# The first four feed-forward units: each second product in a PSUM bank of its own, and weight tiles ordered behind the norm of the second token half

## The chip, the core and the metric

One core of one Trainium2 chip runs the whole program in one launch. The metric is device microseconds for one execution. The profile is one execution taken by the hardware profiler; its times count from the first instruction.

## What is computed

One residual block of a streaming encoder over 512 tokens of width 1024, in float32:

```python
xn = rmsnorm(h, norm_mix_g)
u  = xn @ w_in                                  # q, k, v, rnn_x, rnn_gate, gate_a, gate_b
ya = chunked_band_attention(q, k, v, rel_table) @ w_attn_out
yb = (rg_lru(conv(xr)) * gelu(gr)) @ w_rnn_out
h  = h + (g_a * ya + g_b * yb) @ w_o
hn = rmsnorm(h, norm_ffn_g)
g, up = split(hn @ w_ffn_in)                    # 1024 -> 2 x 2816
h  = h + (silu(g) * up) @ w_ffn_out
out = rmsnorm(h, final_norm_g)
```

## The kernel before

Every matrix product is done on values split into a high part (rounded to the matmul's type, by a ScalarE copy) and a low part (the rest, by a VectorE subtraction): `mm3` issues three matmuls, high by high, high by low, low by high (lines 76, 77, 78).

The products with `w_ffn_in` are cut further, in the manner of Strassen and Winograd. A *unit* is 256 columns of the output (named fg0, fu0, fg2, fu2, fg4, ...; g is the gate half, u the other). Its weight block gives four quarter blocks and four sums of them (a11, a12, a22, s1 to s4 are the seven used); the normed activations give quarter blocks b11, b21, b22 and four sums t1 to t4. A unit is then seven *products* of 512 by 128 by 256, each twelve matmuls of 128 x 128 x 256, in place of eight.

Units from fg4 on go one after the other through `block_product`. The first four (fg0, fu0, fg2, fu2; `ahead_names`) go side by side: first a11 b11 and a12 b21 for each of the four, then s4 b22 for the four, then s1 t1, s2 t2, s3 t3, a22 t4, four products each time. This lets TensorE begin on b11 and b21, which need the first half of the tokens alone, while the second half is still being normed. I write s4(2) for the product s4 b22 of the third of these units, counted from 0. For each of the four units `firsts` holds a PSUM tile p, in which a11, s2, s3 and a22 accumulate, and an SBUF tile c of the four quarters of its output. The products a12, s4 and s1 go to another PSUM tile q and are taken from there into c.

*PSUM.* There are eight banks; the pools give four to the tag `mm` (the p tiles), two to the tag `t` and two to the tag `s`. `of_pair` gives one q tile of `s`, one bank, to two units: the first unit writes the left half of that bank and the second the right half. A write to a bank waits until the reads of that bank which come before it in the program are over. The tag `t` serves the transposes of `turned`.

*Weight tiles.* The sums s1 to s4 of the first four units were written to HBM earlier. `first_tile` loads the parts of two units (a *pair*, 0 or 1) into one of three `raw` buffers by two DMAs on SyncE's queue (line 1068), copies the high part on ScalarE (L1070) and makes the low part on VectorE (L1071). The high and low parts lie in a `whl` buffer; four of these are in the pool `wp`, and the a11 and a12 blocks of the four units (one buffer a unit) hold all four until their products are done. `first_pair("s4", 0, ...)` and `first_pair("s4", 1, ...)` have places of their own (`sums_room`, `x32p`). I write s1/0 for the tile of s1 of pair 0.

*The norm and the turn.* `square_h`, `summed_h` and `scaled_h` make the normed rows xs of a token tile (sum of squares, square root on ScalarE at L1048, reciprocal and scaling on VectorE at L1053 and L1055); tiles 0 and 1 are the first token half, 2 and 3 the second. `turned(xs, jp, ...)` transposes two feature tiles of two token tiles into one bank of tag `t` (PE, L324) and reads them out: high part on ScalarE (L329), low part on VectorE (L330), and the plain values x32, half on each (L332, L334). For the second half, jp 0 and 2 give x32 alone, and jp 4 and 6 give b22 and x32. `right_sum` splits a sum t1 to t4 into its parts `bt` (L82, L83).

*Order.* In this part TensorE's instructions are issued in the order of the program text (`manual_schedule`). The other engines' queues are ordered by a planner that walks the program with its own model of times and takes, of what it thinks ready, the earliest in the text. `tc.issue_after(ins)` puts the instructions traced inside it, those on the engine of `ins`, behind `ins` in that engine's queue; it sets an order there and no wait on another engine.

Of the kernel before, what the change touches and what calls it, by code (L numbers as in the profile page):

```python
# [8 lines left out]
F32 = mybir.dt.float32  # L9
F32R = mybir.dt.float32r  # L10
AF = mybir.ActivationFunctionType
ALU = mybir.AluOpType
PSUM = bass.MemoryType.PSUM

P = 128
D = 1024
# [20 lines left out]
def block_kernel(ctx: ExitStack, tc: tile.TileContext, x, norm_mix_g, w_in, b_merge, rel_table,  # L37
# [3 lines left out]
    pe, dve, act, pool, sp = nc.tensor, nc.vector, nc.scalar, nc.gpsimd, nc.sync  # L41
# [4 lines left out]
    def opened(name, bufs=1, side="left"):  # L46
        st = ExitStack()
        return st, st.enter_context(pool_of(name, bufs, side))
# [14 lines left out]
    ps = ctx.enter_context(tc.tile_pool(name="ps", bufs=2, space=PSUM, reuse_waits="tile"))  # L63
# [4 lines left out]
    def f(ap):  # L68
        return ap.bitcast(F32)

    def mm_tile(name, tag="mm"):
        return ps.tile([P, S], F32, tag=tag, bufs=4 if tag == "mm" else 2, name=name)
# [22 lines left out]
    ahead_names = strassen[:4]  # L95
# [187 lines left out]
    eps_t = cp.tile([P, 1], F32, name="eps_t")  # L283
    dve.memset(eps_t[:], EPS)
    warm = cp.tile([P, 1], F32, name="warm")
# [7 lines left out]
    for n, w in enumerate((w_rg_r, w_rg_i)):  # L293
        pairs = w.rearrange("(t two) d e -> two d t e", two=2)
        for e in range(2):
            at = slice(HD * (n ^ e), HD * (n ^ e) + HD)
# [23 lines left out]
    def turned(xs, jp, g, dst, half, name, whole_of=None):  # L320
        pt = ps.tile([P, 2, 256], F32, tag="t", bufs=2, name=f"pt_{name}{half}_{jp}")
        for i in range(2):
            for j in range(2):
                pe.transpose(pt[:, j, i * P:(i + 1) * P], xs[i][:, (jp + j) * P:(jp + j + 1) * P], ident[:])  # L324
        for j in range(2):
            jj = jp + j
            hi, lo = dst(jj, 0, half), dst(jj, 1, half)
            if hi is not None:
                act.activation(hi, pt[:, j], AF.Identity, scale=g[:, jj:jj + 1])  # L329
                dve.scalar_tensor_tensor(lo, pt[:, j], g[:, jj:jj + 1], f(hi), ALU.mult, ALU.subtract)  # L330
            if whole_of and j == 0:
                act.activation(whole_of(jj, half), pt[:, j], AF.Identity, scale=g[:, jj:jj + 1])  # L332
            elif whole_of:
                dve.tensor_scalar(whole_of(jj, half), pt[:, j], g[:, jj:jj + 1], None, ALU.mult)  # L334

    def norm_half(pl, src, ssq, g, dst, half, name):
        xs = [scaled(pl, src, ssq, name, 2 * half + i)[0] for i in range(2)]
        for jp in range(0, KT, 2):
            turned(xs, jp, g, dst, half, name)
# [52 lines left out]
    gf = vc[:, V_GF:V_GF + 8]  # L392
# [244 lines left out]
    ss = ctx.enter_context(tc.tile_pool(name="ss", bufs=2, space=PSUM, reuse_waits="tile"))  # L637
# [244 lines left out]
    with tc.manual_schedule(engines={mybir.EngineType.PE}):  # L882
        chain, second = ([mm_tile(f"pv_{tag}{i}", tag) for i in range(2)] for tag in ("mm", "t"))
# [107 lines left out]
    for j in range(KT):  # L991
# [6 lines left out]
        at = lo_half if j % 4 < 2 else slice(0, S)  # L998
# [9 lines left out]
    ht = [zp.tile([P, D], F32, tag="z", name=f"h{t}") for t in range(NT)]  # L1008
# [25 lines left out]
            dve.scalar_tensor_tensor(hs, bank_of(2 * half + i, cc)[:], 0.5, hs, ALU.mult, ALU.add)  # L1034

    hsq, q2s = [], {}

    def square_h(t, cc):
        if t not in q2s:
            q2s[t] = cp.tile([P, 2], F32, tag="hsq2", bufs=2, name=f"hsq2_{t}")  # L1040
        junk = tg_.tile([P, S], F32, tag="tg", name=f"hj{t}_{cc}")
        act.activation(junk[:], ht[t][:, cc * S:(cc + 1) * S], AF.Square, accum_out=q2s[t][:, cc:cc + 1])

    def summed_h(t):
        q = cp.tile([P, 1], F32, tag="ssq", bufs=4, name=f"hsq{t}")
        dve.tensor_reduce(q[:], q2s[t][:], mybir.AxisListType.X, ALU.add)
        sd = cp.tile([P, 1], F32, tag="sd", bufs=4, name=f"sd_ffn{t}")
        act.activation(sd[:], q[:], AF.Sqrt, bias=eps_t[:], scale=1.0 / D)  # L1048
        return sd

    def scaled_h(t, sd):
        rs = cp.tile([P, 1], F32, tag="rs", bufs=4, name=f"rs_ffn{t}")
        dve.reciprocal(rs[:], sd[:])  # L1053
        o = x32p.tile([P, D], F32, tag="xs", bufs=2, name=f"xs_ffn{t}")
        dve.tensor_scalar(o[:], ht[t][:], rs[:, 0:1], None, ALU.mult)  # L1055
        return o

    def finish_h(t, cc):
# [5 lines left out]
    def first_tile(pl, tag, bufs, low, keys, srcs):  # L1064
        name = "_".join(keys[0])
        raw = wp.tile([P, 2, 4, P], F32, tag="raw", bufs=3, name=f"raw_{name}")
        for i, src in enumerate(srcs):
            sp.dma_start(out=raw[:, i], in_=src)
        o = pl.tile([P, 2, 2, 4, P], F32R, tag=tag, bufs=bufs, name=f"whl_{name}")
        act.activation(o[:, :, 0], raw[:], AF.Copy)  # L1070
        low.tensor_sub(o[:, :, 1], raw[:], f(o[:, :, 0]))  # L1071
        for i, key in enumerate(keys):
            first_w[key] = o[:, i]

    def first_block(name, half, kh):
        col = chunks[index[name]][1][0][1] + half * P
        return w_ffn_in[kh * S:(kh + 1) * S, col:col + P].rearrange("(k p) e -> p k e", p=P)
# [4 lines left out]
    def first_pair(key, of, pl=None, bufs=4):  # L1082
        at = ("s2", "s1", "s3", "s4", "a22").index(key)
        names = ahead_names[2 * of:2 * of + 2]
        first_tile(pl or wp, "whl", bufs, dve, [(name, key) for name in names],
                   [first_block(name, 1, 1) if key == "a22" else first_sums[name][at // 2][:, at % 2] for name in names])
# [36 lines left out]
    x32_stack, x32p = opened("x32", 1, "right")  # L1123
# [10 lines left out]
    sd = [summed_h(0)]  # L1134
    finish_h(1, 1)
    xs = [scaled_h(0, sd[0])]
# [8 lines left out]
    h_read(1, 0, (1, 1), (1,))  # L1145
    square_h(3, 1)
    first_pair("s4", 0, sums_room, 1)
    first_pair("s4", 1, x32p, 1)
    h_multiply("a22", "t4", 1, 0, False, (0,))
    turned(xs, 4, gf, hn_at, 0, "ffn", f_at)  # L1150
    finish_h(2, 0)
# [2 lines left out]
    xs = [scaled_h(2, summed_h(2))]  # L1154
# [25 lines left out]
    def of_x(kh, half, i):  # L1180
        return x32[2 * kh + i][:, :, half * 256:half * 256 + 256]

    def halves_of(dst, op, in0, in1):
        for i in range(2):
            op(dst[:, 2 * i:2 * i + 2], in0(i), in1(i))

    def own_half(t):
        return lambda i: t[:, 2 * i:2 * i + 2]
# [11 lines left out]
    def first_product(n, to, a, b, start):  # L1200
        product(to, first_w[ahead_names[n], a], right_of(b), start)

    def of_pair(key):
        both = []

        def at(n):
            if n % 2 == 0:
                both[:] = [ss.tile([P, 2, 256], F32, tag="s", bufs=2, name=f"q_{key}_{ahead_names[n]}")]
            return both[0][:, n % 2]
        return at  # L1210

    def copied(o, src):
        act.activation(o, src, AF.Copy)

    bt = []

    def right_sum(t):
        o = btp.tile([P, 2, 4, 256], F32R, name=f"bt{len(bt)}")
        split(o[:, 0], o[:, 1], t[:])
        bt.append(o)  # L1220

    second = of_pair("a12")
    for n, (p_, c_) in enumerate(firsts.values()):
        first_product(n, p_[:], "a11", "b11", True)
        copied(c_[:, 0], p_[:])
        if n == 2:
            for jp in (4, 6):
                turned(xs, jp, gf, hn_at, 1, "ffn", f_at)
        q_ = second(n)
        first_product(n, q_, "a12", "b21", True)  # L1230
        dve.tensor_add(c_[:, 0], q_, c_[:, 0])
        if n == 1:
            act.activation(warm[:], xs[1][:, 0:1], AF.Silu)
            for jp in (0, 2):
                turned(xs, jp, gf, hn_at, 1, "ffn", f_at)
            t1 = sums("t1")
            halves_of(t1, dve.tensor_sub, lambda i: of_x(0, 1, i), lambda i: of_x(0, 0, i))
            right_sum(t1)
            first_pair("s1", 0)
        elif n == 2:  # L1240
            first_pair("s1", 1)
    t2, t3, t4 = (sums(f"t{i}") for i in range(2, 5))
    halves_of(t2, dve.tensor_sub, lambda i: of_x(1, 1, i), own_half(t1))
    right_sum(t2)
    first_pair("s2", 0)
    halves_of(t3, dve.tensor_sub, lambda i: of_x(1, 1, i), lambda i: of_x(0, 1, i))
    right_sum(t3)
    first_pair("s2", 1)
    halves_of(t4, dve.tensor_sub, lambda i: of_x(1, 0, i), own_half(t2))
    right_sum(t4)  # L1250
    hn_right = right_side(lambda kh, half, part, k: bl[kh, half][:, part, k], bt)
# [5 lines left out]
        dve.tensor_mul(o, o, u)  # L1257

    for key, right in (("s4", "b22"), ("s1", "t1")):
        into = of_pair(key)  # L1260
        for n, (p_, c_) in enumerate(firsts.values()):
            q_ = into(n)
            first_product(n, q_, key, right, True)
            if key == "s4":
                copied(c_[:, 1], q_)
            else:
                copied(c_[:, 3], q_)
                dve.tensor_add(c_[:, 1], q_, c_[:, 1])
# [82 lines left out]
    for j in range(4, FT, 2):  # L1351
# [5 lines left out]
        g, u = (sc.tile([P, 4, 256], F32, tag=f"c{w}", name=f"c_{w}{j}") for w in "gu")  # L1357
        block_product(f"fg{j}", 0, hn_right, g)
        o = act_tile(j)[:].rearrange("p a b -> p (a b)")
# [11 lines left out]
    op = ctx.enter_context(pool_of("out", 4, "right"))  # L1371
# [128 lines left out]
    with tc.manual_schedule(engines={mybir.EngineType.PE, mybir.EngineType.DVE, mybir.EngineType.Activation}):  # L1500
# [40 lines left out]
        most, last = range(len(units) - 1), [len(units) - 1]  # L1541
# [43 lines left out]
```

## Time and profile before

| | |
|---|---|
| time, median of 3 runs | 859.81 us (858.61 to 859.98) |
| the profiled execution | 860.57 us, span 858.7 us, mean granted clock 0.996 |
| busy share of the span | PE 98%, weight loads 86%, VectorE 79%, ScalarE 60%, GpSimd 20% |
| first product a11(0) starts | 515.09 us |
| a11 of fg4, the first after the four units' 28 products | 563.75 us |

In the timeline views a row is: start in us, duration in us, engine, line, operation, what it writes and reads, count; in brackets, the idle time of the engine ahead of it and the instruction that ended this idle time. Tile names come without numbers: `p_fg` and `p_fu` are the p tiles, `q_a_fg` is a q tile of a12 and `q_s_fg` one of s4 or s1 (named after the pair's first unit), `whl_fg_s` a weight tile of sums, `c_fg` the quarters. A matmul's duration is longer than the step to the next, since matmuls overlap; its end is modelled, so steps are taken from start to start.

### The profile page before, as it was taken

What the parts mean: (1) busy time and instruction counts of PE and PEld (TensorE: products, weight loads), DVE (VectorE), ACT (ScalarE), POOL (GpSimd) and SP (SyncE); (2) the same over time, 40 slices, a digit from 0 to 9 for tenths busy, and PEclk for the clock granted to TensorE, in tenths of its full rate; (3) what the DMA queues carried; (4) which work ended last, traced back from release to release, by engine and by line L of the source; (5) the groups of instructions that cost most, each with busy time, mean ns of one, the idle gap of its engine ahead of it and who ended that gap; (6) DMA issues with size and microseconds to landing.
All of it is one profiled execution on the core that took longest, in us unless ns stands there. A gap on an engine that the chain in (4) does not pass through costs nothing.

```text
span 858.7 us, 13173 instructions
## 1 busy us (share of the span) xinstructions
PE 840.6 (98%) x4836; PEld 734.9 (86%) x4836; DVE 678.3 (79%) x1029; ACT 514.6 (60%) x878; POOL 174.6 (20%) x192
## 2 busy tenths in 40 slices
PE   8999999999999999999999998899999999999997
PEld 5977887888888888888888888899999999988885
DVE  5799767698676777756578888698999987699985
ACT  7578686723565777656555557455565565385554
POOL 2234302220022576755400220000000001000002
PEclk9999999999999999999999999999999999999998
DMA  8584331694556246644467442474756332886622
GB/s 271 179 314 173 98 98 58 219 352 155 180 157 215 74 148 213 205 133 150 147 220 245 130 141 75 147 270 154 287 193 225 106 118 88 280 299 209 203 73 99
DMA packets 117776, 152.48 MB, mean 178 GB/s; under 512 B 7632, under 2 KB 86080, under 8 KB 117712
## 3 DMA queue, kind: packets, MB, share of 16 engines
q1 hardware_dynamic: 114032, 143.98, 51.2%
q10 hardware_dynamic: 3680, 7.67, 3.0%
q8 instruction: 38, 0.62, 0.3%
q14 instruction: 26, 0.21, 0.1%
HBM read 126.42 MB, written 25.21 MB: 177 GB/s over the span
## 4 chain that ended last, share of the span: by engine, by line
PE 84%; DVE 6%; POOL 3%; ACT 3%; issue 2%; DMA 2%; ACTq 0%; SPq 0%; DVEq 0%; POOLq 0%
PE po_out L76 4%; PE po_out L78 4%; PE po_out L77 4%; PE p_fg L76 2%; PE p_fg L78 2%; PE p_fg L77 2%; PE p_fu L76 2%; PE p_fu L78 2%; PE p_fu L77 2%; POOL p L717 2%; PE po_gb L76 2%; PE po_gb L77 2%; PE po_k L76 2%; PE po_gb L78 2%; PE po_k L78 2%
## 5 line engine op out<-in xcount | busy, mean ns | idle before, releaser
L717 POOL TENSOR_SCALAR p<-p,rl 128x128 f32<-128x128 f32 (+1 forms) x64 | 49.0, 785 | 123.2 <-DVE rl L715 123.1
L1299 POOL TENSOR_TENSOR act_lo<-act,act_hi 128x1024 fp32r<-128x1024 f32 x1 | 2.4, 2408 | 221.3 <-ACT act_hi L1298 221.3
L712 ACT ACTIVATE p<-p,m 128x128 f32<-128x128 f32 (+1 forms) x64 | 35.7, 561 | 9.7 <-DVE m L711 9.5
L83 DVE TENSOR_TENSOR pp<-pT,pp 128x384 fp32r<-128x384 f32 (+1 forms) x48 | 28.5, 598 | 15.7 <-ACT pp L82 15.4
L83 DVE TENSOR_TENSOR whl_t<-raw_t,whl_t 128x1024 fp32r<-128x1024 f32 x26 | 31.6, 1217 | 0.3 <-ACT whl_t L82 0.3
L711 DVE CUSTOM_DVE_ANT_0 p<-s,bias 128x128 f32<-128x128 f32 (+1 forms) x64 | 29.5, 483 | 0.2
L1496 POOL TENSOR_TENSOR h<-h,g_fin 128x512 f32<-128x512 f32 x4 | 5.1, 1291 | 117.8 <-ACT oj L1492 117.8
L77 PE MATMUL po_xr<-xnT,whl_xr 128*128 128x512 f32 (+1 forms) x80 | 28.4, 360 | 0.0
L82 ACT ACTIVATE whl_t<-raw_t 128x1024 fp32r<-128x1024 f32 x26 | 27.2, 1047 | 1.5 <-PE po_h L78 1.5
L76 PE MATMUL po_gr<-xnT,whl_gr 128*128 128x512 f32 (+1 forms) x80 | 28.1, 352 | 0.0
L76 PE MATMUL po_xr<-xnT,whl_xr 128*128 128x512 f32 (+1 forms) x80 | 27.2, 359 | 0.6 <-ACT xnT L329 0.6
L78 PE MATMUL po_xr<-xnT,whl_xr 128*128 128x512 f32 (+1 forms) x80 | 27.7, 350 | 0.0
L78 PE MATMUL po_gr<-xnT,whl_gr 128*128 128x512 f32 (+1 forms) x80 | 27.5, 348 | 0.1
L77 PE MATMUL po_gr<-xnT,whl_gr 128*128 128x512 f32 (+1 forms) x80 | 27.6, 346 | 0.0
L76 PE MATMUL po_ga<-xnT,whl_ga 128*128 128x512 f32 x64 | 25.4, 396 | 0.3 <-DVE oacc L752 0.3
L76 PE MATMUL po_gb<-xnT,whl_gb 128*128 128x512 f32 x64 | 25.3, 395 | 0.2 <-DVE xc L470 0.2
L83 DVE TENSOR_TENSOR whl_fg_s<-s_fg,whl_fg_s 128x1024 fp32r<-128x1024 f32 x18 | 21.8, 1222 | 4.5 <-ACT whl_fg_s L82 4.3
L77 PE MATMUL po_gb<-xnT,whl_gb 128*128 128x512 f32 x64 | 25.2, 393 | 0.0
L76 PE MATMUL po_q<-xnT,whl_qk 128*128 128x512 f32 x64 | 25.1, 393 | 0.0
L78 PE MATMUL po_ga<-xnT,whl_ga 128*128 128x512 f32 x64 | 25.1, 392 | 0.0
L78 PE MATMUL po_q<-xnT,whl_qk 128*128 128x512 f32 x64 | 25.0, 390 | 0.0
L76 PE MATMUL po_k<-xnT,whl_qk 128*128 128x512 f32 x64 | 25.0, 390 | 0.0
(511 smaller groups left out, 3345.3 us busy)
## 6 DMA issues: line engine op xcount, KB each, us to landing
raw_t<-sums SPq DMA_DIRECT2D x20, 512.0 KB, 4.4
raw_fu<-in_w_ffn_in_dram SPq DMA_DIRECT2D x18, 512.0 KB, 3.6
raw_fg<-in_w_ffn_in_dram SPq DMA_DIRECT2D x18, 512.0 KB, 3.7
raw_qk<-in_w_in_dram SPq DMA_DIRECT2D x32, 256.0 KB, 3.4
raw_b<-in_w_ffn_out_dram SPq DMA_DIRECT2D x15, 512.0 KB, 4.6
spillf<-in_w_ffn_out_dram SPq DMA_DIRECT2D x12, 512.0 KB, 6.5
sums<-spillf SPq DMA_DIRECT2D x12, 512.0 KB, 2.7
raw_xr<-in_w_in_dram SPq DMA_DIRECT2D x8, 512.0 KB, 4.5
```

The source lines that it names most:

```text
L76: pe.matmul(o, sh, mh, start=start, stop=False, skip_group_check=parts)
L77: pe.matmul(o, sh, ml, start=False, stop=False, skip_group_check=parts)
L78: pe.matmul(o, sl, mh, start=False, stop=stop, skip_group_check=parts)
L82: act.activation(hi, src, AF.Copy)
L83: dve.tensor_sub(lo, src, f(hi))
L711: dve.tensor_tensor_reduce(prob[qb][:], scs[qb], bias[:, S - w:S], -1.0, 3e38, ALU.add, ALU.min, nmax[:, qb:qb + 1])
L712: exp = act.activation(prob[qb][:], prob[qb][:], AF.Exp, bias=nmax[:, qb:qb + 1], scale=-1.0, accum_out=lsum[:, qb:qb + 1])
L717: pool.tensor_scalar(prob[qb][:], prob[qb][:], rl[:, qb:qb + 1], 1.0, ALU.mult, ALU.mult)
L1299: pool.tensor_sub(lo[:], o[:], f(hi[:]))
L1496: eng.tensor_mul(hs, hs, g_fin[:, cc * S + at.start:cc * S + at.stop])
```

## The change

- `of_pair` goes. `half_bank` gives each product's q a tile of 128 x 256, in a bank of its own: for a12 the two banks of tag `s` in turn; for s4 and s1 the tags `s` and `t` in turn, which makes four banks in rotation.
- The transposes of jp 4 and 6 for the second token half go from between a11(2) and a12(2) to behind a12(2).
- The one-element Silu that loads ScalarE's table is traced with unit 0 in place of unit 1.
- The tiles s4/1 and s1/0 are traced behind unit 0's a12 and queued behind the square root (ScalarE) and the scaling (VectorE) of token tile 3. s4/1 was traced ahead of the last products of `h`, s1/0 behind t1.
- The tiles s1/1, s2/0 and s2/1 are queued behind the last high part of the turn (ScalarE) and the second half of the sum t2 (VectorE).
- `turned`, `copied`, `halves_of`, `summed_h` and `scaled_h` hand back the instruction that the queueing needs.

```diff
@@ turned
+                last = act.activation(hi, pt[:, j], AF.Identity, scale=g[:, jj:jj + 1])
...
+                last = act.activation(whole_of(jj, half), pt[:, j], AF.Identity, scale=g[:, jj:jj + 1])
...
+        return last
@@ summed_h, scaled_h
-        act.activation(sd[:], q[:], AF.Sqrt, bias=eps_t[:], scale=1.0 / D)
+        last_scaled[:] = [act.activation(sd[:], q[:], AF.Sqrt, bias=eps_t[:], scale=1.0 / D)]
...
-        dve.tensor_scalar(o[:], ht[t][:], rs[:, 0:1], None, ALU.mult)
+        last_scaled.append(dve.tensor_scalar(o[:], ht[t][:], rs[:, 0:1], None, ALU.mult))
@@ -1145,7 +1147,6 @@
     first_pair("s4", 0, sums_room, 1)
-    first_pair("s4", 1, x32p, 1)
     h_multiply("a22", "t4", 1, 0, False, (0,))
@@ -1200,17 +1202,12 @@
-    def of_pair(key):
-        both = []
-
-        def at(n):
-            if n % 2 == 0:
-                both[:] = [ss.tile([P, 2, 256], F32, tag="s", bufs=2, name=f"q_{key}_{ahead_names[n]}")]
-            return both[0][:, n % 2]
-        return at
+    def half_bank(key, n, tags="s"):
+        tag = tags[n % len(tags)]
+        return (ss if tag == "s" else ps).tile([P, 256], F32, tag=tag, bufs=2, name=f"q_{key}_{ahead_names[n]}")[:]
@@ -1219,33 +1216,36 @@
-    second = of_pair("a12")
     for n, (p_, c_) in enumerate(firsts.values()):
         first_product(n, p_[:], "a11", "b11", True)
         copied(c_[:, 0], p_[:])
-        if n == 2:
-            for jp in (4, 6):
-                turned(xs, jp, gf, hn_at, 1, "ffn", f_at)
-        q_ = second(n)
+        if n == 0:
+            act.activation(warm[:], xs[1][:, 0:1], AF.Silu)
+        q_ = half_bank("a12", n)
         first_product(n, q_, "a12", "b21", True)
         dve.tensor_add(c_[:, 0], q_, c_[:, 0])
-        if n == 1:
-            act.activation(warm[:], xs[1][:, 0:1], AF.Silu)
+        if n == 0:
+            with tc.issue_after(last_scaled[0].ins), tc.issue_after(last_scaled[1].ins):
+                first_pair("s4", 1, x32p, 1)
+                first_pair("s1", 0)
+        elif n == 1:
             for jp in (0, 2):
                 turned(xs, jp, gf, hn_at, 1, "ffn", f_at)
             t1 = sums("t1")
             halves_of(t1, dve.tensor_sub, lambda i: of_x(0, 1, i), lambda i: of_x(0, 0, i))
             right_sum(t1)
-            first_pair("s1", 0)
         elif n == 2:
-            first_pair("s1", 1)
+            for jp in (4, 6):
+                last_turned = turned(xs, jp, gf, hn_at, 1, "ffn", f_at)
     t2, t3, t4 = (sums(f"t{i}") for i in range(2, 5))
-    halves_of(t2, dve.tensor_sub, lambda i: of_x(1, 1, i), own_half(t1))
+    with_t2 = halves_of(t2, dve.tensor_sub, lambda i: of_x(1, 1, i), own_half(t1))
     right_sum(t2)
-    first_pair("s2", 0)
+    with tc.issue_after(last_turned.ins), tc.issue_after(with_t2.ins):
+        first_pair("s1", 1)
+        first_pair("s2", 0)
+        first_pair("s2", 1)
     halves_of(t3, dve.tensor_sub, lambda i: of_x(1, 1, i), lambda i: of_x(0, 1, i))
     right_sum(t3)
-    first_pair("s2", 1)
@@ -1257,9 +1257,8 @@
     for key, right in (("s4", "b22"), ("s1", "t1")):
-        into = of_pair(key)
         for n, (p_, c_) in enumerate(firsts.values()):
-            q_ = into(n)
+            q_ = half_bank(key, n, "st")
             first_product(n, q_, key, right, True)
```

More of the change, by code (lines that the diff above doesn't have):

```diff
@@ L328, in turned @@
             if hi is not None:
-                act.activation(hi, pt[:, j], AF.Identity, scale=g[:, jj:jj + 1])
+                last = act.activation(hi, pt[:, j], AF.Identity, scale=g[:, jj:jj + 1])
                 dve.scalar_tensor_tensor(lo, pt[:, j], g[:, jj:jj + 1], f(hi), ALU.mult, ALU.subtract)
             if whole_of and j == 0:
-                act.activation(whole_of(jj, half), pt[:, j], AF.Identity, scale=g[:, jj:jj + 1])
+                last = act.activation(whole_of(jj, half), pt[:, j], AF.Identity, scale=g[:, jj:jj + 1])
             elif whole_of:
                 dve.tensor_scalar(whole_of(jj, half), pt[:, j], g[:, jj:jj + 1], None, ALU.mult)
+        return last
     def norm_half(pl, src, ssq, g, dst, half, name):
@@ L1036, in block_kernel @@
     hsq, q2s = [], {}
+    last_scaled = []
     def square_h(t, cc):
@@ L1184, in halves_of @@
         for i in range(2):
-            op(dst[:, 2 * i:2 * i + 2], in0(i), in1(i))
+            last = op(dst[:, 2 * i:2 * i + 2], in0(i), in1(i))
+        return last
     def own_half(t):
@@ L1201, in first_product @@
         product(to, first_w[ahead_names[n], a], right_of(b), start)
-    def of_pair(key):
-        both = []
-        def at(n):
-            if n % 2 == 0:
-                both[:] = [ss.tile([P, 2, 256], F32, tag="s", bufs=2, name=f"q_{key}_{ahead_names[n]}")]
-            return both[0][:, n % 2]
-        return at
+    def half_bank(key, n, tags="s"):
+        tag = tags[n % len(tags)]
+        return (ss if tag == "s" else ps).tile([P, 256], F32, tag=tag, bufs=2, name=f"q_{key}_{ahead_names[n]}")[:]
     def copied(o, src):
-        act.activation(o, src, AF.Copy)
+        return act.activation(o, src, AF.Copy)
     bt = []
```

## The prediction

> **What bounds the kernel now.** I read the page's busy shares first, then TensorE's waits around the four units, then the time-ordered rows there, engine by engine, and last the table by stage.
>
> ```profile
> span 858.7 us, 13173 instructions
> PE 840.6 (98%) x4836; PEld 734.9 (86%) x4836; DVE 678.3 (79%) x1029; ACT 514.6 (60%) x878; POOL 174.6 (20%) x192
> ```
>
> TensorE is the bound, so a change pays what it takes out of TensorE's row. Its waits, by what ended them: first in the stretch 515 to 564 us (the 28 products), then just ahead of it, then from 564 us to the end:
>
> ```profile
> PE q_s_fg L76 <- DVE c_fg L1268: 2.5, 2, 1.6
> PE q_s_fg L76 <- ACT c_fg L1213: 1.7, 2, 1.2
> PE pt_ffn L324 <- DVE x L334: 0.9, 1, 0.9
> ...
> PE pt_ffn L324 <- DVE xs_ffn L1055: 0.3, 1, 0.3
> ...
> PE q_fu L76 <- ACT keepb_fu L252: 0.4, 1, 0.4
> ```
>
> Six waits that the change may touch, and hardly any after them: behind this stretch TensorE has almost no slack in which an early arrival could get lost by a wait that is already there. TensorE's rows, in order of time:
>
> ```profile
> 515.09 0.28 PE L76 MATMUL p_fg<-hn,whl_fg_a 128*128 128x256 f32 x1
> ...
> 520.84 1.04 PE L324 MATMUL pt_ffn<-ident,xs_ffn 128*128 128x128 f32 x8
> 521.63 0.36 PE L76 MATMUL p_fg<-hn,whl_fg_a 128*128 128x256 f32 x1
> ...
> 523.02 0.28 PE L78 MATMUL p_fg<-hn,whl_fg_a 128*128 128x256 f32 x1
> 524.15 1.09 PE L324 MATMUL pt_ffn<-ident,xs_ffn 128*128 128x128 f32 x8 [0.86 <-DVE x L334]
> ...
> 530.72 0.28 PE L78 MATMUL q_s_fg<-hn,whl_fg_s 128*128 128x256 f32 x1
> 531.48 0.38 PE L76 MATMUL q_s_fg<-hn,whl_fg_s 128*128 128x256 f32 x1 [0.47 <-ACT c_fg L1213]
> ...
> 534.32 0.28 PE L78 MATMUL q_s_fg<-hn,whl_fg_s 128*128 128x256 f32 x1
> 535.80 0.39 PE L76 MATMUL q_s_fg<-hn,whl_fg_s 128*128 128x256 f32 x1 [1.20 <-ACT c_fg L1213]
> ...
> 538.66 0.28 PE L78 MATMUL q_s_fg<-bt,whl_fg_s 128*128 128x256 f32 x1
> 539.87 0.39 PE L76 MATMUL q_s_fg<-bt,whl_fg_s 128*128 128x256 f32 x1 [0.93 <-DVE c_fg L1268]
> ...
> 542.72 0.28 PE L78 MATMUL q_s_fg<-bt,whl_fg_s 128*128 128x256 f32 x1
> 544.58 0.39 PE L76 MATMUL q_s_fg<-bt,whl_fg_s 128*128 128x256 f32 x1 [1.58 <-DVE c_fg L1268]
> ...
> 563.75 0.28 PE L76 MATMUL p_fg<-hn,whl_fg_a 128*128 128x256 f32 x1
> ...
> 567.71 0.28 PE L76 MATMUL p_fu<-hn,whl_fu_a 128*128 128x256 f32 x1
> ```
>
> Four products run from 515.09 to 520.84: 1.44 us each, 0.12 us a matmul. The four stops at 531.48, 535.80, 539.87 and 544.58 stand ahead of s4(1), s4(3), s1(1) and s1(3): each is the second unit of a pair, whose q is the other half of a bank that ScalarE or VectorE still reads for the first. The reader should see that each stop is a sharing of a bank, and not a lack of data; how long it lasts is set by the queue in which the reading instruction stands:
>
> ```profile
> 533.48 2.00 ACT L82 ACTIVATE bt<-sum_t 128x1024 fp32r<-128x1024 f32 x2
> 535.38 0.38 ACT L1213 ACTIVATE c_fg<-q_s_fg 128x256 f32<-128x256 f32 x1
> ...
> 503.94 1.22 DVE L1071 TENSOR_TENSOR whl_fg_s<-raw_fg_s,whl_fg_s 128x1024 fp32r<-128x1024 f32 x1
> ...
> 522.48 1.23 DVE L1071 TENSOR_TENSOR whl_fg_s<-raw_fg_s,whl_fg_s 128x1024 fp32r<-128x1024 f32 x1 [0.95 <-ACT whl_fg_s L1070]
> 523.62 0.87 DVE L334 TENSOR_SCALAR x<-pt_ffn,vc 128x256 f32<-128x256 f32 x2
> ...
> 528.98 0.47 DVE L330 SCALAR_TENSOR_TENSOR hn<-pt_ffn,vc,hn 128x256 fp32r<-128x256 f32 x1
> ...
> 532.10 0.42 DVE L1231 TENSOR_TENSOR c_fu<-q_a_fg,c_fu 128x256 f32<-128x256 f32 x1
> ...
> 535.98 3.49 DVE L83 TENSOR_TENSOR bt<-sum_t,bt 128x1024 fp32r<-128x1024 f32 x3
> 539.39 0.42 DVE L1268 TENSOR_TENSOR c_fg<-q_s_fg,c_fg 128x256 f32<-128x256 f32 x1
> ...
> 542.97 1.23 DVE L1071 TENSOR_TENSOR whl_fg_s<-raw_fg_s,whl_fg_s 128x1024 fp32r<-128x1024 f32 x1 [0.52 <-ACT whl_fg_s L1070]
> ...
> 564.86 1.28 DVE L83 TENSOR_TENSOR whl_fu_a<-raw_fu,whl_fu_a 128x512 fp32r<-128x512 f32 x2
> ...
> 569.54 1.21 DVE L581 TENSOR_TENSOR spillf<-spillf,spillf 128x1024 f32<-128x1024 f32 x1
> ```
>
> The copy at 535.38 stood behind two splits of 2.00 us; the add at 539.39 behind three of 3.49 us; the third L1268 behind the low part at 542.97. At 523.62 the read-out that frees the transposes' bank stood behind the low part at 522.48.
>
> **The change, part by part.** The sum is made against the profiled execution's own time, 860.57 us, of which the span is 858.7.
>
> *q in banks of their own.* No instruction is added, removed or resized. For s4 and s1 the banks go round by four, so a product's bank was last used four products earlier: its reader has three products, 4.3 us, before anyone needs the bank. The longest delays above (2.0 and 3.5 us) fit in that. By steps from start to start, less 0.12, the stops cost 0.64, 1.36, 1.09 and 1.74 us, and the first matmul after a stop lasts 0.38 or 0.39 against 0.28, about 0.10 more each time: 4.83 + 0.40 = 5.23 us gained. Bounds: 5.23 if the readers keep within 4.3 us; 0 if later data put the same stops back (rivals). I take 5.23, since both longest delays are under 4.3.
>
> *The transposes of jp 4, 6 behind a12(2).* They start 1.44 us later on TensorE, at 524.6 instead of the 523.1 at which they could have begun. Their bank was free at 524.1 (the first of the two read-outs at 523.62), so the stop (524.15 - 523.02 - 0.12 = 1.01 us) goes even if s1/0 takes the place that the low part at 522.48 had. What is late next is b22 itself: its last low part ran at 528.98 with the transposes at 524.15; it is wanted by the last three matmuls of s4(0), which in the new order starts at 515.09 + 8 x 1.44 + two turns of 0.87 (0.79, and a slow first matmul) = 528.3, so at 529.4. Transposes 0.4 us later put that part's end at 529.4 + 0.4 = 529.8: 0.4 us short. With the split of t1 ordered behind it, 0; with another weight tile in front of it, 1.2 more. I take 0.2.
>
> *s4/1 out of the first half's chain.* The low part at 503.94 stood between the norms of token tiles 0 and 1, and TensorE waited 0.3 us for the scaled tile 1. That goes, 0.3 gained; the bound is 0.3 too, since nothing else waits there. The tile then stands behind the scaling of tile 3, near 519.4. It is first read by s4(2), at 531.2 in the new order: cover of more than 10 us.
>
> *s1/0 beside it* is read by s1(0) at 534.1, split near 521 to 524: covered. *s1/1, s2/0, s2/1 behind the turn and t2.* Their DMAs are held by no queue edge, but by the ring of three `raw` buffers, and move with the low parts that free them:
>
> ```profile
> 505.19 0.32 SPq L1068 DMA_DIRECT2D raw_fg_s<-sums_fg  x1
> ...
> 520.61 0.32 SPq L1068 DMA_DIRECT2D raw_fg_s<-sums_fg  x1
> ```
>
> The first of these two is s2/0's load; it slips to about 520.6, because s4/1 keeps its buffer until then, and two others slip with it to about 523 (s2/1) and 532 (s3/0). SyncE issues nothing else in between, and GpSimd has no part in it. s2/0 is split near 530, s3/0's place falls free at 537, after s1(1), and it is read at 545.6: covered by 5 us and more. On VectorE the three low parts cost 3 x 1.14, two of them as before and one, s1/1, new behind t2. The first of the splits that start at 535.98, that of t2, ended near 537.1; one tile more puts it near 538.3, and s2(0) wants it at 539.8. Covered by 1.5 us, as far as the plan puts t2 ahead of t3 and t4.
>
> *The add of a12(3)* (532.10, 2.5 us after its product) frees the bank that s4(2) now uses. In the new order a12(3) ends near 528.6 and s4(2) starts at 531.2: the same delay gives 531.5 and a stop of 0.3. Bounds: 0 with the add at once, 1.4 with one more tile ahead of it. I take 0.3, the row's own delay.
>
> *The Silu's table load* moves from unit 1 to unit 0, but it still needs the scaled tile 3; ScalarE does the same work. Nothing.
>
> *What VectorE carries on.* The table by stage:
>
> ```profile
> 515.00:529.40 14.40, 13.54 (x114) 13.29 (x113) 11.99 (x24) 11.65 (x23) 0.00 (x0) 1.00 0.22 73
> 529.40:546.10 16.70, 12.51 (x98) 11.70 (x97) 12.40 (x18) 7.61 (x13) 0.00 (x0) 1.00 0.34 103
> 546.10:563.70 17.60, 17.60 (x149) 17.60 (x148) 15.13 (x24) 10.53 (x16) 0.00 (x0) 1.00 0.55 165
> ...
> 600.00:640.00 40.00, 39.65 (x331) 39.45 (x330) 37.95 (x51) 23.39 (x42) 0.00 (x0) 1.00 0.65 227
> ```
>
> After the length of each stretch come the busy times of TensorE, weight loads, VectorE, ScalarE and GpSimd, then TensorE's clock. VectorE has 11.99 + 12.40 + 15.13 = 39.5 us in the first three, 40.7 with s4/1 moved in, and 48.6 - 6.2 = 42.4 us in which to do it if TensorE gains all. It may idle 1.8 us, where it idled 2.4 in the first stretch alone. Most of its idle time then is gone, and it comes to fg4 and fu4 with a debt of roughly 0.5 to 2 us. The weights of fu4 were ready near 566.1 for a use at 567.71, a slack of 1.6. So the debt mostly fits: 0 at best, 2 at worst; I take 0.5.
>
> *Sum.* 5.23 + 1.01 + 0.30 = 6.54 gained, less 0.2, 0.3 and 0.5: 5.5 us. 860.57 - 5.5 = 855.1. The median of the runs, 859.81, lies 0.76 under the profiled execution, so the median forecast is 854.3.
>
> [...] In the table TensorE's clock is 1.00 in all three stretches, stops of up to 1.58 us included. [...]
>
> **Rivals.**
>
> 1. *VectorE becomes the limit* (partial gain). For: the 1.8 us above, and 37.95 of 40 us at 600 to 640, so a debt is paid back slowly, at 2 us in 40. Against: its work there is needed only some us later. It decides when the debt passes the slack of 1.6 us ahead of fu4. Price: 1.2 to 3.5 us more than I took; a gain of 2.0 to 4.3, a time of 855.5 to 857.8.
>
> 2. *The banks were not it.* If t2's split, s2/0 or s1/1 come so late that TensorE stops ahead of s1(2) or s2(0) for as long as it did before, nothing is gained: s2(0) started near 546.1 (544.58 and one slow product) and would have to start there again, 6.3 us after it could. Against: the three splits were over at 539.5. Time: 859.8.
>
> 3. *Slower.* The planner lays out the three other queues anew, up to the last units, from its own idea of when TensorE frees things. The place: behind fg4, where VectorE has 2.05 us of rest in 40. Price: each spill step (L581, 1.21 us) that comes ahead of a low part for which TensorE is waiting. It decides from six such steps, 7.3 us against a gain of 5.5: 861.6 or more. For: only that this order is not in my hand. Against: 0.4 us of waits in 300 us behind this place.
>
> [...]
>
> **How the numbers follow.** My forecast 0.60, rival 1 0.22, rival 2 0.10, rival 3 0.06, rival 4 0.02. A measurement tells about 0.2%, 1.7 us, from no change. Faster: 0.60, and 0.20 of rival 1, 0.80; same: the rest of rival 1 and rival 2, 0.12; slower: rivals 3 and 4, 0.08. The range goes from 852.8, all 6.54 us and half a microsecond of spread between runs, to 857.9, the end of rival 1; rivals 2 to 4 stay out, 0.18. My forecast's own range is 853.2 to 855.5.
>
> **What would show it.** Right: no stop ahead of s4(1), s4(3), s1(1), s1(3); q rows that alternate between two tags; the first product still near 515 (0.3 earlier), and a11 of fg4 near 558. Each L1268 may then stand late without a stop behind it. [...]

## The result, and the profile after

The changed kernel takes 853.02 us (median of 4 runs, 852.42 to 853.59) against 859.38 us for the kernel before (4 runs, 858.61 to 859.98): a ratio of 0.9926, 95% interval 0.9909 to 0.9944, some 6.4 us faster. 854.3 had been forecast. The runs of one kernel fall into groups about 1.1 us apart (the changed kernel's at 852.4 to 852.5 and at 853.5 to 853.6), so differences of 1 us or less are read from the traces and not from the medians.

The profiled execution of before that the prediction used came to the four units 1.9 us later than another of the same kernel, 1.4 us of it before the first matmul of `po_gb`, a mark near the start (39.13 us in place of 37.73). Its clock was at 0.50 from 11.29 to 14.70 us, where the other shows 1.00. So this second profiled execution of before (858.69 us, span 856.8) is the one that spans are compared with. Line numbers of the changed kernel are up to 7 away from those of before, because lines were added.

The heads of the pages of the changed kernel and of before run again, busy shares:

```profile
span 850.5 us, 13164 instructions
PE 839.3 (99%) x4836; PEld 733.8 (86%) x4836; DVE 676.0 (79%) x1029; ACT 513.8 (60%) x878; POOL 173.3 (20%) x192
```

```profile
span 856.8 us, 13173 instructions
PE 840.1 (98%) x4836; PEld 733.9 (86%) x4836; DVE 676.3 (79%) x1029; ACT 514.2 (60%) x878; POOL 174.1 (20%) x192
```

The work of every engine is the same within 0.8 us; the span is 6.3 us shorter. So idle time of TensorE went, and no work did. Where it went is read from two marks on TensorE: a11(0), and the first matmul of fg4's s1 product, `q_fg<-bt`. The changed kernel first, then before run again: length of each stretch, then busy times of TensorE, weight loads, VectorE, ScalarE, GpSimd, and TensorE's clock:

```profile
512.87:558.62 45.75, 45.25 (x377) 45.03 (x376) 41.19 (x66) 32.11 (x55) 0.00 (x0) 1.00 0.48 151
558.62:850.50 291.88, 285.48 (x1964) 266.62 (x1962) 254.03 (x344) 162.99 (x280) 7.50 (x5) 0.99 0.55 186
```

```profile
513.18:564.36 51.18, 46.13 (x378) 45.11 (x377) 41.50 (x67) 31.96 (x54) 0.00 (x0) 1.00 0.40 126
564.36:856.80 292.44, 285.72 (x1964) 266.73 (x1962) 253.97 (x342) 162.80 (x281) 7.51 (x5) 0.99 0.55 185
```

The four units' stretch loses 5.43 us of its 51.18, the rest 0.56, and a11(0) starts 0.31 earlier: 6.30 together. VectorE does the same 41 us of work in the stretch in either kernel; what shrank is its rest, from 9.7 to 4.6 us.

TensorE's waits in the changed kernel, first from 480 to 560 us; the list from 559 us on is empty:

```profile
PE q_s_fg L77 <- DVE hn L330: 0.5, 1, 0.5
```

Of the waits shown of before none is left, and one is new, inside s4(0). Its row, and VectorE's queue up to it:

```profile
518.64 1.03 PE L324 MATMUL pt_ffn<-ident,xs_ffn 128*128 128x128 f32 x8
522.38 1.04 PE L324 MATMUL pt_ffn<-ident,xs_ffn 128*128 128x128 f32 x8
...
526.49 0.28 PE L76 MATMUL q_s_fg<-hn,whl_fg_s 128*128 128x256 f32 x1
527.27 0.39 PE L77 MATMUL q_s_fg<-hn,whl_fg_s 128*128 128x256 f32 x1 [0.50 <-DVE hn L330]
```

```profile
524.44 0.87 DVE L330 SCALAR_TENSOR_TENSOR hn<-pt_ffn,vc,hn 128x256 fp32r<-128x256 f32 x2
526.39 0.42 DVE L1226 TENSOR_TENSOR c_fu<-q_a_fu,c_fu 128x256 f32<-128x256 f32 x1 [1.08 <-PE q_a_fu L78]
526.74 0.48 DVE L330 SCALAR_TENSOR_TENSOR hn<-pt_ffn,vc,hn 128x256 fp32r<-128x256 f32 x1
```

Both turns now follow their neighbours without a stop. But VectorE stands idle for 1.08 us at 525.3 with b22's third low part next but one in its queue: at the head is the add of a12(3), which waits for TensorE. TensorE then waits for that low part. The stop with its slow restart costs 527.27 - 526.49 - 0.12 = 0.66 us, and two slow first matmuls 0.1 each: about 0.8.

The readers of q are no earlier than before: there the add that reads s1(0) began 0.6 us after its product (539.39, against 538.66 + 0.12). ScalarE's queue at s4(0) and VectorE's at s1(0), changed kernel:

```profile
526.59 2.98 ACT L1072 ACTIVATE whl_fg_s<-raw_fg_s 128x1024 fp32r<-128x1024 f32 x3
529.43 0.41 ACT L1210 ACTIVATE c_fg<-q_s_fg 128x256 f32<-128x256 f32 x1
```

```profile
532.45 2.35 DVE L1073 TENSOR_TENSOR whl_fg_s<-raw_fg_s,whl_fg_s 128x1024 fp32r<-128x1024 f32 x2
534.72 0.68 DVE L1186 TENSOR_TENSOR sum_t<-x,sum_t 128x512 f32<-128x512 f32 x1
535.32 2.35 DVE L83 TENSOR_TENSOR bt<-sum_t,bt 128x1024 fp32r<-128x1024 f32 x2
537.59 0.41 DVE L1267 TENSOR_TENSOR c_fg<-q_s_fg,c_fg 128x256 f32<-128x256 f32 x1
```

s4(0) ends with the start of s4(1), at 528.39, and its copy begins 1.04 us later, behind three high parts. s1(0) ends near 534.2 (528.39 + 4 x 1.44) and is read at 537.59, 3.4 us later, behind tiles and splits. Nobody waits for either, because no product comes back to those banks in that time.

### The profile page after: what moved, and what is told of

Same layout as the page of the kernel before. It is cut to its first block, busy times and chain, and to the rows that moved or that the text cites. A ratio compares the mean times of both kernels' runs of the same rounds, so it can differ in the third digit from the quotient of the medians.

```text
span 850.5 us, 13164 instructions
## 1 busy us (share of the span) xinstructions
PE 839.3 (99%) x4836; PEld 733.8 (86%) x4836; DVE 676.0 (79%) x1029; ACT 513.8 (60%) x878; POOL 173.3 (20%) x192
## 4 chain that ended last, share of the span: by engine, by line
PE 90%; DVE 3%; POOL 3%; ACT 2%; issue 1%; DMA 1%; ACTq 0%; SPq 0%; DVEq 0%; POOLq 0%
PE po_out L76 4%; PE po_out L77 4%; PE po_out L78 4%; PE p_fu L76 3%; PE p_fu L77 2%; PE p_fu L78 2%; PE p_fg L76 2%; PE p_fg L77 2%; PE p_fg L78 2%; POOL p L718 2%; PE po_gb L76 2%; PE po_gb L77 2%; PE po_ya L78 2%; PE po_gb L78 2%; PE po_k L76 2%; PE po_ya L76 2%
## 5 line engine op out<-in xcount | busy, mean ns | idle before, releaser
L78 PE MATMUL po_ya<-aT,whl_ya 128*128 128x512 f32 x64 | 25.0, 390 | 0.0
```

The lines of the kernel that those rows point to most:

```text
L78: pe.matmul(o, sl, mh, start=False, stop=stop, skip_group_check=parts)
```

## The experiments

Theory A: the gain comes from the banks, and what counts is the slack between a product and the next product in its bank, set against the reader's place in its queue. Its rival Q: the gain comes from the weight tiles' new places in the queues, which take them out of the readers' way, and the banks add little. Times of these kernels are compared with before on the same chip (858.57, median of 16, for the first four; 858.66, median of 9, for the others).

**The banks alone** (`banks`), put on the kernel before:

```diff
-    def of_pair(key): ...
+    def half_bank(key, n, tags="s"): ...
-        q_ = second(n)
+        q_ = half_bank("a12", n)
-            q_ = into(n)
+            q_ = half_bank(key, n, "st")
```

> The kernel before with half_bank alone: one bank for each q, four in rotation for s4 and s1; no tile queued anew, the transposes of jp 4 and 6 where they were. Theory A (the four stops are the sharing of a bank): no stop ahead of s4(1), s4(3), s1(1), s1(3); 5.2 us gained, near 854.2; the stop of about 1 us ahead of the transposes and the one of 0.3 us on the scaled tile 1 stay. Theory Q (the stops are the place of the readers in their queues, and the same late queue would stop TensorE elsewhere): new stops ahead of s1 or s2, a gain under 2.5 us, 857 or more.

Measured: 854.05 us (5 runs, 852.80 to 854.13), ratio 0.994 [0.9927, 0.9952]. TensorE has one wait left between 480 us and the end, the transposes' (its row has seven of the eight):

```profile
PE pt_ffn L324 <- DVE x L334: 0.8, 1, 0.8
```

```profile
522.22 0.98 PE L324 MATMUL pt_ffn<-ident,xs_ffn 128*128 128x128 f32 x7 [0.84 <-DVE x L334]
```

a11(0) is at 513.15 and fg4's mark at 559.14: a stretch of 45.99 us, 5.19 less than 51.18. A's four stops were put at 5.23. A holds. By the medians the gain is 4.5 us, by the fastest runs 5.6 (852.80 against 858.43).

**The order and the queues alone** (`order_only`): the changed kernel with q two to a bank again.

```diff
-    def half_bank(key, n, tags="s"): ...
+    def of_pair(key): ...
-        q_ = half_bank("a12", n)
+        q_ = second(n)
-            q_ = half_bank(key, n, "st")
+            q_ = into(n)
```

> The changed kernel with the shared banks of before (of_pair): only the queueing and the place of the transposes. Theory A: the stops ahead of the second units stay, and by the readers' places in the changed kernel (the first L1267 at 537.6 where s1(0) ends near 534.1) the one ahead of s1(1) grows to 3 us or more; a gain of at most 1.5 us, 858 to 861. Theory Q: the order does the work; 4 us or more gained, 855.5 or less.

Measured: 861.02 us (11 runs, 859.65 to 861.98), ratio 1.0022 [1.0014, 1.0031]. Q is refuted: without the banks the rest of the change gains nothing. TensorE's waits, its rows at the stops, and three neighbouring stretches with the clock behind GpSimd's column:

```profile
PE q_s_fg L76 <- DVE c_fg L1274: 2.7, 2, 1.6
PE q_s_fg L76 <- ACT c_fg L1215: 1.8, 2, 1.3
PE q_s_fg L77 <- DVE hn L330: 0.5, 1, 0.5
```

```profile
527.20 0.39 PE L77 MATMUL q_s_fg<-hn,whl_fg_s 128*128 128x256 f32 x1 [0.50 <-DVE hn L330]
...
529.82 0.58 PE L76 MATMUL q_s_fg<-hn,whl_fg_s 128*128 128x256 f32 x1 [1.34 <-ACT c_fg L1215]
530.20 0.42 PE L77 MATMUL q_s_fg<-hn,whl_fg_s 128*128 128x256 f32 x1
530.42 0.41 PE L78 MATMUL q_s_fg<-hn,whl_fg_s 128*128 128x256 f32 x1
```

```profile
526.00:529.80 3.80, 1.98 (x14) 1.56 (x13) 3.47 (x8) 3.77 (x6) 0.00 (x0) 1.00 0.02 4
529.82:533.19 3.37, 3.37 (x15) 3.37 (x16) 3.37 (x5) 2.35 (x3) 0.00 (x0) 0.50 0.23 59
533.20:536.60 3.40, 2.93 (x24) 2.72 (x24) 3.40 (x5) 1.47 (x3) 0.00 (x0) 1.00 0.70 251
```

The four stops stand where they stood before, 4.5 us of waiting in place of 4.2. The one ahead of s4(1) grew from 0.47 to 1.34 us, since three high parts stand ahead of that copy on ScalarE, as in the changed kernel's rows above. The one ahead of s1(1) did not grow to 3 us or more, as theory A had it, but is 1.09 us: the stops before it made TensorE late too, so that s1(0) ends near 537.9 and not near 534.1, and its reader starts at 538.66. Behind the stop ahead of s4(1), the matmuls follow each other every 0.21 us in place of 0.12, for 3.37 us, at a clock of 0.50: 15 of them, some 1.4 us lost. The stretch is 52.73 us (512.80 to 565.53), 1.55 more than before. In this execution that is about what half rate cost, since all waits in the stretch come to 5.0 us in either kernel (before with the transposes' 0.86, this one with the 0.50 in s4(0)). Two of the 11 runs (859.96 and 860.40) have a mean clock of 0.999, which leaves no room for 3.4 us at half rate, and lie above before's median too; why they do is open.

**Two banks in place of four** (`two`): the products no longer share a bank, but s4 and s1 go round the two banks of `s` alone.

```diff
-            q_ = half_bank(key, n, "st")
+            q_ = half_bank(key, n)
```

> The changed kernel with s4 and s1 on the two banks of tag s in turn, each q still alone in its bank. Not sharing is enough (theory A in its narrow form): as the changed kernel, 853.0. Slack counts, not sharing as such: a bank is wanted again after one product, 1.44 us; the copies of s4 are in time, the first L1267 (537.6 in the changed kernel) is not, a stop of 2 to 2.5 us ahead of s1(2), near 855.3.

Measured: 855.8 us (6 runs, 855.5 to 857.0), ratio 0.9967 [0.9955, 0.9979]; the stretch is 49.82 us. VectorE's queue, TensorE's row and its clock behind it:

```profile
535.10 2.35 DVE L83 TENSOR_TENSOR bt<-sum_t,bt 128x1024 fp32r<-128x1024 f32 x2
537.37 0.41 DVE L1267 TENSOR_TENSOR c_fg<-q_s_fg,c_fg 128x256 f32<-128x256 f32 x1
```

```profile
537.84 0.39 PE L76 MATMUL q_s_fg<-bt,whl_fg_s 128*128 128x256 f32 x1 [2.16 <-DVE c_fg L1267]
```

```profile
537.84:541.20 3.36, 3.36 (x17) 3.36 (x18) 2.84 (x4) 0.38 (x1) 0.00 (x0) 0.56 0.64 212
```

The four stops ahead of the second units are gone, and a slack of one product, 1.44 us, covers the readers of s4. A stop of 2.16 us stands in a new place, ahead of s1(2), which takes the bank of s1(0): the reader there starts 3.3 us after that product. So it is the size of the slack that counts and not the sharing of a bank as such. Half rate follows here too, at some 1.5 us more in this execution, which took 856.77 us. Three of the six runs took 855.50 to 855.59, one of them with a mean clock of 0.999, near the 855.3 expected from the stop alone.

**The add of a12(3) behind the low parts** (`add3`): the changed kernel, with this one add queued on VectorE behind b22's last low part.

```diff
-                dve.scalar_tensor_tensor(lo, ...)
+                low[:] = [dve.scalar_tensor_tensor(lo, ...)]
...
+        if n == 3:
+            with tc.issue_after(low[0].ins):
+                dve.tensor_add(c_[:, 0], q_, c_[:, 0])
```

> The changed kernel with the add of a12(3) queued behind the last low part of b22 on VectorE. In the changed kernel VectorE stood idle for 1.08 us at 525.3 with this add at the head of its queue and the low parts of b22 behind it, and TensorE then stopped in s4(0). If that is the cause: no stop in s4(0), 0.8 us gained on the changed kernel, near 852.2. If the low parts are late because the transposes are: as the changed kernel, 853.0.

Measured: 851.52 us (4 runs, 851.47 to 851.68), ratio 0.9916 [0.9902, 0.9929]. No wait of TensorE is left from 480 us to the end. VectorE's queue:

```profile
525.84 0.48 DVE L332 SCALAR_TENSOR_TENSOR hn<-pt_ffn,vc,hn 128x256 fp32r<-128x256 f32 x1 [0.72 <-ACT hn L331]
526.25 0.47 DVE L336 TENSOR_SCALAR x<-pt_ffn,vc 128x256 f32<-128x256 f32 x1
526.64 0.47 DVE L332 SCALAR_TENSOR_TENSOR hn<-pt_ffn,vc,hn 128x256 fp32r<-128x256 f32 x1
527.03 0.47 DVE L336 TENSOR_SCALAR x<-pt_ffn,vc 128x256 f32<-128x256 f32 x1
527.42 0.41 DVE L1230 TENSOR_TENSOR c_fu<-q_a_fu,c_fu 128x256 f32<-128x256 f32 x1
```

The third low part runs at 525.84 in place of 526.74, as soon as ScalarE has made its high part, and the stretch is 45.06 us (512.68 to 557.74), 0.69 less than in the changed kernel. So the new stop in s4(0) came from the add at the head of VectorE's queue. This is the fastest kernel here, ahead of both: its slowest run lies 0.74 us under the fastest of the changed kernel (852.42).

**Both kernels once more** (`before_again`, `after_again`), without an edit:

> The kernel before once more, for its trace. The profiled execution of before ran its first matmuls at a granted clock of 0.66 between 10 and 15 us and reached a later mark 1.5 us after the changed kernel's. If that is chance of one execution: clock 1.00 there now, the mark near 37.6 us, a span near 857, and the stretch of the 28 products again with four stops and 48 to 49 us long. If it belongs to the kernel before: as in its first trace.

> The changed kernel as it is, timed beside the others on this chip. Both theories: about 6 us under the kernel before, 852.4 to 853.6.

Measured: before 858.69 us, with its stretch at 51.18 as the first time and a11(0) at 513.18 in place of 515.09, and with the clock at 1.00 between 10 and 15 us. So the 2 us were of that one execution. The changed kernel 853.32 (5 runs, 852.42 to 853.61), ratio 0.9932 [0.9919, 0.9944], 5.3 us under before by the medians; its stretch is 45.75 us as the first time. The 1.2 us between the two profiled executions lie ahead of a11(0) (514.10 against 512.87); in the first 60 us one wait is in the second and not in the first:

```profile
PE rg L492 <- POOL xch L474: 1.1, 1, 1.1
```

**Without the second queueing** (`noq2`): s1/1, s2/0 and s2/1 are left to the planner.

```diff
-    with tc.issue_after(last_turned.ins), tc.issue_after(with_t2.ins):
-        first_pair("s1", 1)
-        first_pair("s2", 0)
-        first_pair("s2", 1)
+    first_pair("s1", 1)
+    first_pair("s2", 0)
+    first_pair("s2", 1)
```

> The changed kernel with s1/1, s2/0 and s2/1 in the same place of the text but not queued behind the turn and t2. If this queueing carries part of the gain: their low parts stand ahead of the read-outs of the turn (one ahead of x, one ahead of the low parts of b22), the stop in s4(0) grows from 0.5 to 1.5 us or more, near 854. If it does not: as the changed kernel, within 0.5 us.

Measured: 853.77 us (5 runs, 853.58 to 854.93), ratio 0.9946 [0.9932, 0.9959]. TensorE's waits in the stretch and behind it, and VectorE's queue:

```profile
PE q_s_fg L77 <- DVE hn L330: 1.0, 1, 1.0
...
PE q_fu L76 <- ACT keepb_fu L252: 0.4, 1, 0.4
```

```profile
524.15 1.22 DVE L1073 TENSOR_TENSOR whl_fg_s<-raw_fg_s,whl_fg_s 128x1024 fp32r<-128x1024 f32 x1
525.28 0.87 DVE L330 SCALAR_TENSOR_TENSOR hn<-pt_ffn,vc,hn 128x256 fp32r<-128x256 f32 x2
526.07 1.22 DVE L83 TENSOR_TENSOR bt<-sum_t,bt 128x1024 fp32r<-128x1024 f32 x1
527.20 0.42 DVE L1226 TENSOR_TENSOR c_fu<-q_a_fu,c_fu 128x256 f32<-128x256 f32 x1
527.54 0.48 DVE L330 SCALAR_TENSOR_TENSOR hn<-pt_ffn,vc,hn 128x256 fp32r<-128x256 f32 x1
```

A tile is back ahead of the low parts, and the stop in s4(0) is 1.00 us in place of 0.50, less than the 1.5 or more I had put down. The stretch is 0.80 us longer (46.55) and the rest 0.59 (292.47), with the wait at `keepb_fu` back. This queueing is worth 1.4 us by the two profiled executions, 1.2 by the fastest runs and 0.5 to 0.8 by the medians.

**Without the first queueing** (`noq1`): s4/1 and s1/0 traced behind a12(0), but placed by the planner.

```diff
-            with tc.issue_after(last_scaled[0].ins), tc.issue_after(last_scaled[1].ins):
-                first_pair("s4", 1, x32p, 1)
-                first_pair("s1", 0)
+            first_pair("s4", 1, x32p, 1)
+            first_pair("s1", 0)
```

> The changed kernel with s4/1 and s1/0 in the same place of the text but not queued behind the scaled tile 3. If this queueing matters: s4/1 goes back between the norms of tiles 0 and 1, TensorE stops there for 0.3 us again, 0.3 to 0.5 us slower than the changed kernel. If the new place in the text is enough: no difference beyond 0.3 us.

Measured: 852.5 us (5 runs, 852.28 to 854.58), ratio 0.9929 [0.9917, 0.9942], where 0.3 to 0.5 us slower was expected: a miss. s4/1's low part is back between the norms of tiles 0 and 1 (502.00), and from the start of the eight transposes there (504.15) to the next matmul 1.14 us pass in place of 0.80, so a11(0) did come later (513.14). But the stretch is shorter (45.36), and VectorE's queue says why:

```profile
526.27 0.49 DVE L330 SCALAR_TENSOR_TENSOR hn<-pt_ffn,vc,hn 128x256 fp32r<-128x256 f32 x1 [0.98 <-ACT hn L329]
526.67 0.48 DVE L334 TENSOR_SCALAR x<-pt_ffn,vc 128x256 f32<-128x256 f32 x1
527.06 0.41 DVE L1226 TENSOR_TENSOR c_fu<-q_a_fu,c_fu 128x256 f32<-128x256 f32 x1
```

In the planner's new order the add of a12(3) happens to fall behind the third low part, and the stop in s4(0) is gone. This agrees with `add3`. So the first queueing gains its 0.3 us ahead of a11(0), and the order that the planner lays with it loses 0.4 in the stretch: nothing net.

## Why the prediction was right, step by step

*The four stops at shared banks, 5.23.* Right in mechanism and size: 5.19 with the banks alone. The reasoning was by the slack of three products against the longest delay of a reader; two banks, with a slack of one, leave a stop of 2.16 us. What the prediction did not say: the other steps make the readers later, so that they are worth having only on top of the banks (`order_only`).

*The transposes of jp 4 and 6, 1.01.* Their stop is gone from the changed kernel and still there, 0.84, with the banks alone. No kernel moved these transposes alone. In `add3`, where no stop is left, the stretch is 6.12 us shorter than in before, against 5.23 + 1.01 = 6.24.

*s4/1 out of the first half's chain, 0.30.* Counted from the first matmul of `po_gb`, a11(0) comes 0.24 us earlier than in before run again (37.66 to 512.87, against 37.73 to 513.18). The wait of 0.30 itself is listed for the first execution of before alone. But from the first half's transposes to the next matmul 0.80 us pass in the changed kernel, 1.06 in before run again, and 1.14 in `banks` and `noq1`, the three with s4/1's low part between the norms.

*b22's last low parts, 0.2 taken off.* Mis-sized: a stop of 0.50, with its restart about 0.8, and moving one add took 0.69 off the stretch. The cause was not the one given. The prediction looked at the last low part and the last three matmuls of s4(0); the stop is at the fifth matmul, for the third low part. It looked for what would be late, the transposes and the weight tiles; it was an instruction queued ahead of the low parts, which waited at the queue's head for TensorE itself.

*The add of a12(3), 0.3 taken off.* The right instruction and the wrong victim. It ran 0.1 us after its product (526.39), so s4(2) didn't wait for its bank; but by being that prompt it held back b22. The two terms together were put at 0.5 and came to about 0.8.

*VectorE's debt, 0.5 taken off.* Mis-sized: no stop came of it. The stretch kept 4.6 us of rest on VectorE, where 1.8 had been reckoned (42.4 less 40.7 is 1.7). The debt shows only as slack: ahead of fu4 the split of its weights starts at 558.83, two in 1.28 us, for a use at 560.07, so the first is done near 559.5, about 0.6 us early, against 2.2 by the same reckoning in before (564.86 and 567.71). Counted to the end of both, as the prediction did, its slack of 1.6 us is used up (560.11). So the rival that VectorE becomes the limit was nearer than the waits let on; it did not come.

*Nothing was put down for the time behind fg4.* There 0.56 us were gained: the wait at `keepb_fu`, 0.4 with its restart, is gone. It is in both executions of before, in `order_only`, `two` and `noq2`, and absent in the changed kernel, `banks`, `add3` and `noq1`: it goes with the order that the planner lays there. Behind fg4 the queues of ScalarE and VectorE run in one and the same order in all the kernels that have the wait, and in another, but for a few exchanges, in those that do not. Why the first order has it was not tried. This is the place of the rival *slower*, with the other sign.

In sum: 0.24 + 5.43 + 0.56, and 0.07 in the start-up, make the 6.3 us between the two executions; 5.5 were forecast. Of the 0.8 between them, 0.56 were not foreseen, and 0.19 lie in the stretch, where 6.24 gained less 1.0 taken off were forecast and only 0.8 were lost. That the 1.0 taken off came so near the 0.8 is luck: of its three terms one had another cause, one hit another victim and one did not come.

*The clock.* The changed kernel shows 1.00 throughout the stretch: its rotation through four banks did not bring the clock down here. What the chances count as rival 4, at 0.02, eight products at half rate, no run shows. Half rate came in the profiled executions of `order_only` (0.50 over 529.82 to 533.19) and `two` (0.56 over 537.84 to 541.20), at a cost of some 1.4 and 1.5 us, behind a stop of 1.34 us at a shared bank and one of 2.16 us in a rotation through two.

## What to carry to other kernels

For a PSUM bank that is reused, count the slack in products (the number of banks in rotation less one) and set it against the latest place at which the reader can stand in its own in-order queue, not against how long the reading takes: here a slack of three products was worth 5.2 us and a slack of one left a stop of 2.2. When a stop has a reader that comes late, look as well at what is at the head of the reader's queue: an instruction put as early as its data allow can stand there waiting for the very engine that everything behind it has to feed (1.08 us of idle time on VectorE in the changed kernel), and queueing it later cost nothing here (`add3`, 0.69 us off the stretch). Measure the parts of such a change one by one, since an order that gained at most 1 us on top of the banks lost 2.4 without them (medians), and half rate, 0.50 for some 3.4 us, had a part in that loss in the profiled execution.

## What the runs showed of the hardware

The half rate behind a stop was not expected, since stops of up to 1.58 us in before had left the clock at 1.00. The stops after which it came are of 1.34 us (`order_only`, with one of 0.50 shortly ahead) and 2.16 us (`two`). It lasted some 3.4 us each time, from 529.80 and from 538.25, and ended while TensorE worked without a stop. The first execution of before shows 0.50 for as long near its start, from 11.29 to 14.70, and once more from 854.38 to its end, behind the last matmul.

The length of the stop alone does not tell these apart from the stop of 1.58; `order_only` has a stop of 1.58 too, ahead of s1(3), behind which the matmuls follow each other every 0.12 us. What does tell them apart was not shown: no run changed the length of one stop and left the rest as it was.
